# Grouped-query attention on one core: the first load of v issued directly behind the first keys

## The chip, the cores and the metric

The kernel runs on one core of a Trainium2 chip. A core has a matrix engine (TensorE, with a separate row for its weight loads), a vector engine (VectorE), an engine for functions such as exp (ScalarE), a general engine (GpSimd) and one that only issues transfers and waits (SyncE). Each takes its own list of instructions in order; they are tied together by semaphores. Transfers run on 16 DMA engines which all queues share. The metric is the device time of one execution in microseconds; before the change it is 363.3 us, the median of 3 runs (362.96 to 363.51).

## The reference: what is computed

Attention with grouped heads: batch 8, 8 query heads, 2 key and value heads, 1024 positions, head size 64, float32 in and out. Four query heads share one key and value head.

```python
for g in range(n_kv_heads):
    scores = scale * np.matmul(q_group, k_group.transpose(0, 1, 3, 2))
    attn = np.exp(scores - scores_max)
    attn = attn / (np.sum(attn, axis=-1, keepdims=True) + 1e-08)
    output[:, q_start:q_end] = np.matmul(attn, v_group)
```

scale is 1/8, scores_max the maximum of each row.

## The kernel before, in words

**Jobs.** One pair of batch and query head is a job; there are 64, numbered j. A job's scores are computed transposed, in 8 chunks of 128 keys by 1024 queries: two matmuls of 512 columns (L795) fill one PSUM slot `sp` of 128x1024. There are three such slots, so three chunks can be under way.

**Two ways to take the exponential.** Most chunks (378 of 512) go through ScalarE: one instruction (L805) reads a slot and writes exp(scale x score) as bf16 into a tile `pt`. The other 134 go through VectorE, which builds an exponential out of integer operations: a first pass out of PSUM (L816, tile `yt`), then on pairs of chunks the steps L823 (`zt`), L830 (`et`) and L839, with part of L839's columns done by GpSimd (L769). No maximum is subtracted.

**Product with v.** The exponentials are the weights of matmuls against `va`, which holds v as bf16 with a column of ones behind each 64 values, so that the 65th output column is the row sum. L857 does this piece by piece (8 pieces of 128 queries a job); for job 0 alone it goes chunk by chunk (L877), as soon as a chunk's exponential and v are there. Then VectorE takes the reciprocal of the sums (L922) and multiplies (L931), and SyncE stores.

**Where v comes from.** `load_v` (L590) is a transfer on SyncE's queue from v in HBM into a float32 tile `vs`, 256 KB, of which there are two buffers. `place_v` (L595, L596) is a GpSimd copy of `vs` into `va`. There are 16 pairs of batch and key head, so 16 such loads and copies.

**Where q and k come from.** For job 0 they are loaded as float32 by SyncE (k, in two parts, L636 and L638) and by ScalarE's queue (q, L637), cast to bf16 by `place` (L660 on VectorE, L661 on ScalarE), turned by TensorE against an identity (L674, L686) and copied out of PSUM (L691 to L695). For every other job, GpSimd issues a transfer that casts q or k to bf16 in HBM (`cast_q` L563, `cast_k` L576; lines L571 and L579), and SyncE issues a transposing transfer of that into `qt` or `kt` (L614, L604). The casts for jobs 1 to 4 and of the second key head are issued at the start of the kernel, one behind the other.

**What sets the order.** The order of all work is written out beforehand: the class `Plan` plays the engines with fixed costs (the M_ names at the top) and picks, step by step, what TensorE does next. Its list of events, with those for loads and stores sorted in by time, is then emitted, so every engine's list of instructions is fixed before the kernel starts. The plan counts v of job 0 as there at M_V0 = 8000 ns. On TensorE the list begins with idle work on `warm` (L654, L655), the turning of q and k, six chunks of scores of job 0, and then the first 16 products with v (L877); behind these stand the next three chunks of scores, the second of which is the first to read `qt` of job 1.

**Around the change.** The start of the kernel, in program order, is: load k part 1 and part 2 on SyncE with q's load on ScalarE's queue between them, the casting loads of jobs 1 and 2, the idle work, the four `place` casts, and then the first `load_v(0, 0)`. That load carries a dependency added by hand on ScalarE's cast of q:

```python
ins = place(nc.scalar, "q", 0, 2)
...
tc.add_manual_dep(load_v(0, 0).ins, ins.ins.name, Sync, reason="loads in time, not sooner")
```

SyncE's list is therefore: k, k, v, the transposes for jobs 1, 2 and 3, the transpose of the second key head, the second v, and so on. Each transpose waits for its own cast.

Of the kernel before, what the change touches and what calls it, by code (L numbers as in the profile page):

```python
# [486 lines left out]
def kernel(  # L487
# [7 lines left out]
    nc = tc.nc  # L495
# [5 lines left out]
    Sync = mybir.DependencyInfo(mybir.DependencyClass.Sync, mybir.DependencyReason.DATA)  # L501
# [61 lines left out]
    def cast_q(j):  # L563
        b, h = divmod(j, H)
        t = dram.tile([HS, 2 * D], BF16, name=f"qd{j}")
        qd[j] = t
        if j == NJ - 1:
            return nc.gpsimd.dma_start(
                out=t.rearrange("(c p) d -> p c d", p=128), in_=rows(q[b, h], True)
            )  # L570
        return nc.gpsimd.dma_start(  # L571
            out=t.rearrange("(a x) d -> a (x d)", x=4),
            in_=q[b, h].rearrange("(a x) d -> a (x d)", x=8),
        )
# [11 lines left out]
    def rows(x, fours=False):  # L586
        how = "(p c two) d -> p c (two d)" if fours else "(c p two) d -> p c (two d)"
        return x.rearrange(how, p=128, two=2)

    def load_v(b, g):  # L590
        t = vsp.tile([128, NH, 2 * D], FP32, name="vs")
        vs[(b, g)] = t
        return nc.sync.dma_start(out=t, in_=rows(v[b, g], b == g == 0))
# [38 lines left out]
    def load(e, x, lo, hi):  # L632
        src = {"q": q, "k": k}[x][0, 0]
        return e.dma_start(out=f32[x][:, lo:hi], in_=rows(src, True)[:, lo:hi])

    load(nc.sync, "k", 0, 1)  # L636
    load(nc.scalar, "q", 0, NH)  # L637
    load(nc.sync, "k", 1, NH)  # L638
    cast_q(1)
    make_identity(nc, ident)  # L640
    cast_q(2)
# [15 lines left out]
    def place(e, x, lo, hi):  # L657
        to, src = b16[x][:, lo:hi], f32[x][:, lo:hi]
        if e is nc.vector:
            return e.tensor_copy(out=to, in_=src)  # L660
        return e.activation(out=to, in_=src, func=AF.Copy)  # L661

    ins = place(nc.scalar, "q", 0, 2)
    place(nc.vector, "q", 2, NH)
    place(nc.vector, "k", 0, 1)
    place(nc.vector, "k", 1, NH)

    tc.add_manual_dep(load_v(0, 0).ins, ins.ins.name, Sync, reason="loads in time, not sooner")

    s0, s1, s2 = new_slot(0), new_slot(1), new_slot(2)  # L670

# [82 lines left out]
    for when, kind, x, j, c, *cols in ev:  # L754
# [177 lines left out]
        elif kind == "store":  # L932
            b, h = divmod(j, H)
            r = place_of(j * NPIECE)
            ins = nc.sync.dma_start(
                out=rows(out[b, h], j in (0, NJ - 1)),
                in_=ost[:, r : r + NPIECE, :].rearrange("p (s two) d -> p s (two d)", two=2),
            )
# [31 lines left out]
```

The softmax here doesn't subtract the row's maximum and nothing guards it: scores larger than these inputs give would overflow.

## Time and profile before

| what | number |
|---|---|
| time, median of 3 | 363.3 us |
| span of the profiled execution | 362.6 us |
| ScalarE busy | 351.3 us |
| TensorE busy | 350.0 us |
| VectorE busy | 349.8 us |
| GpSimd busy | 125.1 us |
| mean DMA rate | 124 GB/s |

A profile lists for each engine the instructions with their start and length, and for each idle stretch what ended it. A tile is named without its buffer number, so `pt<-sp` is any exp from a PSUM slot. "L805" is line 805 of the kernel. The chain that ended last is followed back from the last instruction, at each step to what released it. DMA queues are numbered: q1 is SyncE's, q10 ScalarE's, q0 GpSimd's casting loads. Busy times of TensorE are modelled from pipelined matmuls and overstate how full it is.

### The profile page before, as it was taken

Reading aid. Unit: us, or ns where it says so; the run is one execution under the profiler, and the core shown is the slowest. Engines: PE = TensorE matmul, PEld = TensorE weight load, DVE = VectorE, ACT = ScalarE, POOL = GpSimd, SP = SyncE. Lnnn points to the kernel's source line nnn. Section 1 sums busy time; section 2 is a strip of 40 time slices with the busy share of each in tenths; the row PEclk is TensorE's granted clock in tenths of the full one; section 3 lists DMA queues with packets and bytes.
Section 4 is the critical chain, followed back from the end, with each engine's and each line's share of the span. In section 5 each row is a group of like instructions: output and inputs, shape, how many; then the busy total and the mean of one; then the engine's idle time right before and its main releaser. Section 6 shows DMA issues by size and latency. Waiting matters only on the chain.

```text
span 362.6 us, 14110 instructions
## 1 busy us (share of the span) xinstructions
PE 350.0 (97%) x6223; PEld 224.6 (62%) x6223; DVE 349.8 (96%) x494; ACT 351.3 (97%) x382; POOL 125.1 (35%) x190
## 2 busy tenths in 40 slices
PE   8789999999999999999999999999999999999995
PEld 3435666666666666656667666666665666666664
DVE  4799999999999999999999999999999999999994
ACT  5799999999999999999999999999999999999995
POOL 3124344353535335342334444244324343421000
PEclk9899999999999999999999999999999999999999
DMA  8625666656668849668466976757488456655132
GB/s 162 117 47 98 128 136 148 119 119 132 134 149 103 169 112 120 140 121 170 111 116 98 171 150 130 125 119 150 107 107 168 110 116 121 149 144 104 47 89 89
DMA packets 89404, 44.82 MB, mean 124 GB/s; under 512 B 46000, under 2 KB 87600, under 8 KB 88112
## 3 DMA queue, kind: packets, MB, share of 16 engines
q1 hardware_dynamic: 86208, 33.44, 41.0%
q0 software_dynamic: 2992, 10.23, 21.1%
q8 instruction: 48, 0.79, 0.9%
q10 hardware_dynamic: 144, 0.26, 0.2%
q14 instruction: 12, 0.10, 0.1%
HBM read 25.17 MB, written 27.00 MB: 144 GB/s over the span
## 4 chain that ended last, share of the span: by engine, by line
DVE 82%; ACT 5%; PE 4%; issue 4%; DMA 2%; POOL 0%; DVEq 0%
DVE yt L816 39%; DVE zt L839 14%; DVE et L830 10%; DVE ost L931 9%; DVE zt L823 9%; ACT pt L805 5%; DVE rec L922 2%; PE sp L795 2%; PE ops L857 2%; DMA vs<-in_v_dram 2%; DMA q<-in_q_dram 1%; PE sp L897 1%; PE ops L877 0%; POOL va L596 0%; ACT q L661 0%
## 5 line engine op out<-in xcount | busy, mean ns | idle before, releaser
L805 ACT ACTIVATE pt<-sp 128x1024 bf16<-128x1024 f32 x378 | 348.7, 1044 | 3.6 <-PE sp L795 3.3
L795 PE MATMUL sp<-qt,kt 64*128 64x512 bf16 x1024 | 174.1, 385 | 5.1 <-ACT pt L805 1.5
L857 PE MATMUL ops<-va,pt 128*128 128x65 bf16 x2928 | 175.9, 194 | 0.0
L816 DVE TENSOR_SCALAR yt<-sp 128x1024 uint16<-128x1024 f32 x134 | 162.8, 1215 | 3.3 <-PE sp L795 3.3
L857 PEld LDWEIGHTS <-pt 128*128 128x128 bf16 x2928 | 130.8, 97 | 33.0 <-issue 33.0
L857 PE MATMUL ops<-va,zt 128*128 128x65 bf16 x1040 | 125.7, 194 | 0.0
L857 PE MATMUL ops<-va,et 128*128 128x65 bf16 x1008 | 119.5, 194 | 0.1
L769 POOL TENSOR_TENSOR zt<-yt,zt 128x320 bf16<-128x320 bf16 x90 | 71.2, 791 | 120.1 <-DVE zt L839 32.9
L857 PEld LDWEIGHTS <-et 128*128 128x128 bf16 x1008 | 81.2, 98 | 21.4 <-issue 21.0
L857 PEld LDWEIGHTS <-zt 128*128 128x128 bf16 x1040 | 84.8, 97 | 10.2 <-issue 10.2
L795 PEld LDWEIGHTS <-kt 64*128 64x128 bf16 x1024 | 48.9, 93 | 57.1 <-issue 36.2
L839 DVE TENSOR_TENSOR zt<-yt,zt 128x1408 bf16<-128x1408 bf16 (+1 forms) x67 | 66.2, 988 | 0.0
L571 POOL DMA_DIRECT2D qd<-in_q_dram x62 | 36.1, 582 | 43.1 <-PE sp L795 39.8
L823 DVE TENSOR_SCALAR zt<-yt 128x2048 uint16<-128x2048 uint16 x67 | 46.2, 690 | 0.4
L830 DVE TENSOR_SCALAR et<-yt 128x2048 uint16<-128x2048 uint16 x67 | 45.5, 679 | 0.0
L931 DVE TENSOR_TENSOR ost<-ops,rec 128x448 f32<-128x448 f32 (+2 forms) x73 | 44.4, 609 | 0.4
L596 POOL CAST va<-vs 128x512 bf16<-128x512 f32 x16 | 10.0, 628 | 28.6 <-DVE ost L931 8.8
L922 DVE RECIPROCAL rec<-ops 128x7 f32<-128x7 f32 (+2 forms) x73 | 14.2, 195 | 0.0
L579 POOL DMA_DIRECT2D kd<-in_k_dram x15 | 8.6, 570 | 11.5 <-PE sp L795 11.5
L649 PE MATMUL ops<-warm 128*128 128x128 bf16 (+1 forms) x63 | 9.2, 265 | 1.2 <-DVE warm L559 1.2
L649 PEld LDWEIGHTS <-warm 128*128 128x128 bf16 x63 | 4.5, 104 | 7.1 <-issue 5.9
L877 PE MATMUL ops<-va,pt 128*128 128x65 bf16 x48 | 2.6, 221 | 2.2 <-POOL va L596 2.2
(37 smaller groups left out, 26.7 us busy)
## 6 DMA issues: line engine op xcount, KB each, us to landing
out_dram<-ost SPq DMA_DIRECT2D x64, 256.0 KB, 3.1
qd<-in_q_dram POOLq DMA_DIRECT2D x63, 128.0 KB, 3.5
vs<-in_v_dram SPq DMA_DIRECT2D x16, 256.0 KB, 3.2
kd<-in_k_dram POOLq DMA_DIRECT2D x15, 128.0 KB, 3.1
kt<-kt SPq DMA_DIRECT2D x30, 64.0 KB, 2.9
qt<-qd SPq DMA_TRANSPOSE x63, 3.9
q<-in_q_dram ACTq DMA_DIRECT2D x1, 256.0 KB, 3.0
kt<-kd SPq DMA_TRANSPOSE x15, 3.8
```

Of the source, the lines that this page charges most:

```text
L571: return nc.gpsimd.dma_start(out=t.rearrange("(a x) d -> a (x d)", x=4), in_=q[b, h].rearrange("(a x) d -> a (x d)", x=8),)
L649: nc.tensor.matmul(ops[bank][:, lo : lo + cols], lhsT=warm[:, 0:128], rhs=warm[:, 0:cols], start=not beside, stop=True, skip_group_check=b ...
L769: gps = nc.gpsimd.tensor_tensor(out=z, in0=flat(yt[j])[:, c, 1024 - GC :], in1=z, op=ALU.mult)
L795: now = nc.tensor.matmul(sps[x][:, half, :], lhsT=t[lo : lo + D, c // NH, ci % NH * 128 : (ci % NH + 1) * 128], rhs=qt[j][lo : lo + D, 0, ...
L805: exps.append(nc.scalar.activation(out=p, in_=where_s[(j, c)], func=AF.Exp, scale=scale))
L816: vec = nc.vector.tensor_scalar(out=yt[ch][:, i, :, :], in0=where_s[c], scalar1=EXP_A, scalar2=EXP_B, op0=ALU.mult, op1=ALU.add,)
L823: vec = nc.vector.tensor_scalar(out=zt[j][:, 0:c], in0=yt[j][:, 0:c], scalar1=0x7F, scalar2=0x3F00, op0=ALU.bitwise_and, op1=ALU.bitwise_or,)
L830: vec = ins = nc.vector.tensor_scalar(out=et[j][:, 0:c], in0=yt[j][:, 0:c], scalar1=0x7F80, scalar2=None, op0=ALU.bitwise_and,)
L839: vec = nc.vector.tensor_tensor(out=z, in0=flat(yt[j])[:, 0:c, 0 : cols[0]], in1=z, op=ALU.mult)
L857: nc.tensor.matmul(ops[plan.group_of[x] % 2][:, lo : lo + D + 1], lhsT=p[:, qs * 128 : (qs + 1) * 128], rhs=va[:, b * G + h // HPG, ci % N ...
L922: vec = nc.vector.reciprocal(out=to, in_=sums)
L931: vec = nc.vector.tensor_tensor(out=to, in0=o, in1=by, op=ALU.mult)
```

## The change

The first load of v is moved up in the program, directly behind the second load of k on SyncE's queue, and loses its dependency on ScalarE's cast. It has nothing left to wait for. The dependency held the load back so that it would not share the DMA engines with the loads of q and k; the change gives that up to have v sooner.

```diff
     load(nc.sync, "k", 0, 1)
     load(nc.scalar, "q", 0, NH)
     load(nc.sync, "k", 1, NH)
+    load_v(0, 0)
     cast_q(1)
     make_identity(nc, ident)
     cast_q(2)
...
-    ins = place(nc.scalar, "q", 0, 2)
+    place(nc.scalar, "q", 0, 2)
     place(nc.vector, "q", 2, NH)
     place(nc.vector, "k", 0, 1)
     place(nc.vector, "k", 1, NH)
-
-    tc.add_manual_dep(load_v(0, 0).ins, ins.ins.name, Sync, reason="loads in time, not sooner")
```

One line fewer: behind L668 every line of the changed kernel has a number smaller by one, and between L639 and L667 the numbers are larger by one.

## The prediction

> **What bounds the kernel now.** I first read the instructions of ScalarE in order of time, because its 351.3 us busy of a 362.6 us span is the largest share. Columns: start, length, engine and line, operation, count, and in brackets the idle time before the stretch with what ended it.
>
> ```profile
> 3.77 0.42 ACT L661 ACTIVATE q<-q 128x256 bf16<-128x256 f32 x1 [1.34 <-DMA q<-in_q_dram]
> ...
> 6.43 3.77 ACT L805 ACTIVATE pt<-sp 128x1024 bf16<-128x1024 f32 x4 [0.62 <-PE sp L795]
> 12.66 47.25 ACT L805 ACTIVATE pt<-sp 128x1024 bf16<-128x1024 f32 x51 [2.46 <-PE sp L795]
> 60.12 297.99 ACT L805 ACTIVATE pt<-sp 128x1024 bf16<-128x1024 f32 x323 [0.20 <-PE sp L795]
> ```
>
> Four exps run, then ScalarE stands still from 10.20 to 12.66, and after that it works without a hole (0.20 us at 60) until 358.1. So the span is the time of the first exp, plus 378 exps back to back at about 0.92 us, plus one hole of 2.46 us, plus a short end. Only the start and that hole can be shortened. VectorE has a hole at the same place: its pass at 13.09 waited 2.57 us for scores, after work that ended at 10.51.
>
> Second, the chain that ended last, in order of time (start, length, what), says where the hole comes from:
>
> ```profile
> 0.74 3.02 DMA q<-in_q_dram
> 3.75 0.02 issue
> 3.77 0.43 ACT q L661
> 4.20 0.02 issue
> 4.22 5.90 DMA vs<-in_v_dram
> 10.11 0.05 issue
> 10.17 0.83 POOL va L596
> 11.00 0.04 issue
> 11.04 1.04 PE ops L877 x16
> 12.08 0.99 PE sp L795 x3
> 13.07 0.02 issue
> 13.09 1.23 DVE yt L816
> ```
>
> The load of the first v tile is issued at 4.22, after ScalarE's first cast, lands 5.9 us later, GpSimd copies it into va, and only then can TensorE run its first 16 products with v (L877). TensorE takes its instructions in order, and behind those 16 stand the next score matmuls (L795) that both ScalarE and VectorE are waiting for.
>
> Third, the waits by engine (total us, times, longest), the first two from the first 45 us, the last from SyncE's own queue, give the sizes:
>
> ```profile
> POOL va L596 <- DMA vs<-in_v_dram: 5.8, 1, 5.8
> ...
> PE ops L877 <- POOL va L596: 2.2, 1, 2.2
> ```
> ```profile
> SPq L593 <- ACT q L661: 2.6, 1, 2.6
> ```
>
> SyncE sat 2.6 us on the dependency that the change removes; TensorE stood 2.23 us before L877, from 8.81 to 11.04.
>
> Fourth, the DMA queues between 5.5 and 7 us (packets, MB, share of the 16 engines):
>
> ```profile
> q0 software_dynamic: 45, 0.19, 101.0%
> ```
>
> q1, SyncE's queue with v on it, moves nothing here although v was issued at 4.22: only q0 does, GpSimd's casting loads (q of heads 1 to 4 and the second k, 128 KB written each). In half-microsecond windows q1's first packets after k come between 7.0 and 7.5. This is why v needed 5.9 us where q and k needed 3.0 and 3.2.
>
> **What the Trainium skill says.** DMA: Bandwidth & Descriptors, section Queues, rings and completion order: an engine takes the descriptors of one ring in order and goes round between the rings that have work, by packets. The trace agrees on the order (v, then the transposes behind it) but shows v kept out for some two microseconds rather than served in turn. The same page, Issuing engines are not separate DMA queues: all queues run on the same 16 engines, so v's bytes are not free wherever they go; the windows from 2 to 4 us show three queues at once, 318 GB/s together. SBUF — State Buffer, section Who interferes with whom: a VectorE instruction with at most one SBUF input outside the two-port modes doesn't contend with GpSimd. The trace agrees: GpSimd's copy of the second v tile at 22.18 lies beside a PSUM pass at 22.04 that takes its usual 1.22 us.
>
> **The change part by part.** Instruction order on all five engines is the same in both kernels; the only difference is that SyncE's third DMA, v, no longer waits for ScalarE.
>
> *Issue of v.* SyncE's two k loads take 0.88 us from 0.74, so v goes out at about 1.62 instead of 4.22: 2.6 us earlier.
>
> *Landing of v.* The trace doesn't show a v load there, so I bound it. Best: 3.0 us as for k and q, landing at 4.6. Worst: 5.9 us again, landing at 7.5. I take about 5.3: v's packets stand directly behind k's in the ring, and k's last pass shortly before 4.0, when the casts have moved only 16 packets; 256 KB at 318 GB/s are 0.8 us, some more for the shared engines. GpSimd is idle from 4.39, its copy is 0.83 us plus 0.1 of hand-over, so va is there at 6.2 (5.5 to 8.4). TensorE wants it at 8.81. Even at the worst bound the whole 2.23 us wait is gone.
>
> *What comes after on TensorE.* 16 products need about 0.5 us at full clock (the third set, at 15.00, was followed by the next work at 15.51), so scores could start at 9.35. Their PSUM slot is freed by the third exp, at 6.43 + 3 x 0.94 = 9.25. From pair start to exp start it took 0.65 us at 12.01, at a granted clock of 0.5; so the fifth exp's scores are ready by 10.0, before ScalarE ends the fourth at 10.20. ScalarE's hole is closed: minus 2.46 us. VectorE's next pass needs the second pair of scores, which can't begin before VectorE's own pass from 8.56 ends at 9.79, and is ready at about 10.3, before VectorE is free at 10.51: its hole closes too. The granted clock, 0.5 between 11 and 13 us after the wait, should also stay at 1, but nothing more is gained by that, for ScalarE never waits again.
>
> *The next input.* That second pair is the first to read qt of head 1, so its transposing load must have landed by 9.8 to 10. Before, it was issued at 4.90 and landed after 5.8 us, at 10.7, standing behind v in the same ring. Now v is out of its way, but the casting load that feeds it (issued 1.25, landed 4.85) shares the engines with v. If v costs it its whole 0.8 us, the transpose goes out at 5.7 and can move when the casts thin out, at about 8; 954 small packets went through from 10 to 11 us, and a transpose has 576 (4032 of under 512 B in the first 30 us, 7 transposes), so one takes some 0.6 us. I take 9.5, bounds 8.2 and 11.5. Head 2's transpose landed at 11.2 and is wanted at about 13.4; later loads are tied to score matmuls and move with them. These cost nothing.
>
> *What v costs at the start.* The first exp depends on q and k. q's 144 packets are all gone by 3.5, before v can move much, and k stands ahead of v in the ring. So the loss is nearly nothing, at worst v's 0.8 us. I take 0.15.
>
> *GpSimd's copy* moves from 10.17 to about 5.3, beside VectorE's casts L692 to L695 and its first pass L816. All read PSUM, and the pass at 22.04 shows such a pass unharmed: nothing.
>
> *Sum.* 2.46 - 0.15 = 2.3 us off a path on which ScalarE has no slack: 363.3 - 2.3 = 361.0, 0.64% less.
>
> **The rivals.**
> 1. *Head 1's qt takes v's place.* For it: it landed at 10.7 before, later than it will be wanted. Against: much of that was v ahead of it. Landing at 10.7 again, the sixth exp's scores, third in TensorE's order, are ready at about 10.7 + 0.45 + 0.2 = 11.35 where ScalarE ends the fifth at 11.12: a hole of 0.2 (VectorE 0.6), so 361.2 to 361.6. At 11.5 it is 1.0: 362.0.
> 2. *k or q is held up* by v's full 0.8 us: 2.46 - 0.8 = 1.7, 361.6. Against: the order in the ring.
> 3. *The gain is given back later*, by loads or buffers that then come late: 363.3. Against: ScalarE's two later stretches show 0.20 us of waiting in 345; everything that feeds it is issued relative to work that shifts along.
> 4. *Slower.* v in front delays k and q by 0.8 and, through the casts, head 1's qt by more than the 2.46 us saved, to beyond 13: no gain and a later start, 363.3 + 0.8 = 364.1. For it: DMA engines are loaded from 2.5 to 11 us. Against: five casts were through by 9.6, and v adds 0.8 us of engine time.
>
> **How the numbers follow.** Forecast 0.65, rival 1 0.18, rival 2 0.06, rival 3 0.06, rival 4 0.05. The forecast itself reaches from 363.3 - 2.46 - 0.2 (the small hole at 60) - 0.3 (spread of the runs of before) = 360.3 up to 361.3; taking in rivals 1 and 2 to 361.9 leaves little over 0.1 outside. Faster by over 0.2% (below 362.57): 0.65 + 0.18 + 0.06 = 0.89; within: 0.06; slower: 0.05.
>
> **What would show it right or wrong.** Right: v issued near 1.6 and landed before 8; no wait of L877 for L596; ScalarE's stretch from about 6.5 going on through 12.66 without a hole over 0.2; first exp at 6.4 to 6.7; the granted clock at 1 from 10 to 14. Wrong by rival 1: a hole of ScalarE or VectorE between 10 and 12 with TensorE waiting at L795 for the load of qt. By rival 2: the casts L660 and L661 later than 3.77 and 3.98. By rival 3: new waits of L805 beyond 13 us. By rival 4: both of the first, and more than 2.5 us of them.

## The result and the profile after

The changed kernel takes 361.1 us (median of 4, 360.94 to 361.45) against 363.36 us before, a ratio of 0.9941 with a 95% interval from 0.9923 to 0.9958. Timed once more in more rounds (first experiment below) it is 0.9945 (0.9933 to 0.9957): 2.0 us less, between 1.6 and 2.4.

ScalarE's instructions of the changed kernel in order of time:

```profile
3.94 0.42 ACT L662 ACTIVATE q<-q 128x256 bf16<-128x256 f32 x1 [1.50 <-DMA q<-in_q_dram]
...
6.29 50.71 ACT L804 ACTIVATE pt<-sp 128x1024 bf16<-128x1024 f32 x55 [0.32 <-PE sp L794]
57.21 297.98 ACT L804 ACTIVATE pt<-sp 128x1024 bf16<-128x1024 f32 x323 [0.20 <-PE sp L794]
```

The 4 and the 51 exps have become one stretch of 55: the hole of 2.46 us is gone, and the small one of 0.20 us has moved from 60.12 to 57.21. q came 0.17 us later than before (3.94 for 3.77), and yet the first exp started 0.14 us earlier (6.29 for 6.43); the first experiment says why.

The chain that ended last, first 10 us of the changed kernel (start, length, what):

```profile
0.74 3.18 DMA q<-in_q_dram
3.91 0.02 issue
3.94 0.43 ACT q L662
4.36 0.05 issue
4.41 0.71 PE sp L673 x5
5.12 0.32 PE ops L673 x3
5.44 0.51 PE ops L685 x8
5.95 0.02 issue
5.98 0.69 DVE kt L694
6.67 1.14 DVE yt L815
7.81 0.04 issue
7.85 0.41 PE sp L794 x2
8.26 0.02 issue
8.28 1.24 DVE yt L815
```

Neither v nor va stands in it any more; it runs from the load of q through the turning of q and k straight into the work. In the waits of the first 45 us (total us, times, longest) nobody waits for L596 now, and the input next in line, the transposed q of head 1, shows a single wait of 0.2 us:

```profile
POOL va L596 <- DMA vs<-in_v_dram: 1.3, 1, 1.3
...
PEld L794 <- DMA qt<-qd: 0.2, 1, 0.2
```

How v got through is in the DMA queues between 4.5 and 5 us of the changed kernel (packets, MB, share of 16 engines):

```profile
q1 hardware_dynamic: 93, 0.18, 94.5%
q0 software_dynamic: 8, 0.03, 32.3%
```

v is 128 packets of 2 KB. Here they pass between 4.0 and 5.5, most of them in the half microsecond shown, in which only 8 of GpSimd's casting packets (q0) start. Before, they passed between 7.0 and 10.

### The profile page after: what moved, and what is told of

It reads as the page before. It is cut to its first block, busy times and chain, and to the rows that moved or that the text cites. A ratio compares the mean times of both kernels' runs of the same rounds, so it can differ in the third digit from the quotient of the medians.

```text
span 359.6 us, 14110 instructions
## 1 busy us (share of the span) xinstructions
PE 348.5 (97%) x6223; PEld 224.1 (62%) x6223; DVE 349.7 (97%) x494; ACT 351.1 (98%) x382; POOL 124.6 (35%) x190
## 4 chain that ended last, share of the span: by engine, by line
DVE 71%; ACT 19%; PE 4%; issue 4%; DMA 1%; DVEq 0%
DVE yt L815 34%; ACT pt L804 19%; DVE zt L838 12%; DVE et L829 8%; DVE ost L930 7%; DVE zt L822 7%; DVE rec L921 2%; PE ops L856 2%; PE sp L794 2%; DMA q<-in_q_dram 1%; PE sp L896 1%; PE sp L673 0%; DVE kt L694 0%; PE ops L685 0%; ACT q L662 0%
## 5 line engine op out<-in xcount | busy, mean ns | idle before, releaser
L856 PE MATMUL ops<-va,pt 128*128 128x65 bf16 x2928 | 176.0, 194 | 0.0
L856 PEld LDWEIGHTS <-zt 128*128 128x128 bf16 x1040 | 84.8, 97 | 10.2 <-issue 10.2
L822 DVE TENSOR_SCALAR zt<-yt 128x2048 uint16<-128x2048 uint16 x67 | 46.2, 689 | 0.4
L596 POOL CAST va<-vs 128x512 bf16<-128x512 f32 x16 | 9.8, 614 | 24.1 <-DVE ost L930 8.8
L843 DVE TENSOR_TENSOR zt<-et,zt 128x2048 bf16<-128x2048 bf16 x3 | 3.7, 1221 | 0.0
```

What stands on the lines that cost most here:

```text
L822: vec = nc.vector.tensor_scalar(out=zt[j][:, 0:c], in0=yt[j][:, 0:c], scalar1=0x7F, scalar2=0x3F00, op0=ALU.bitwise_and, op1=ALU.bitwise_or,)
L856: nc.tensor.matmul(ops[plan.group_of[x] % 2][:, lo : lo + D + 1], lhsT=p[:, qs * 128 : (qs + 1) * 128], rhs=va[:, b * G + h // HPG, ci % N ...
```

## The experiments

Each ratio is against the kernel before as it ran beside the experiment on the same chip: 363.65 us for the changed kernel again and the experiments on the casts, on v's lateness and on v's wait, 363.67 us for the other four timed ones.

### The changed kernel again

No edit.

> The changed kernel once more, timed in more rounds and with a second profile. My theory: the hole of ScalarE (2.46 us) is all there is, so the time is 361.1 again, ratio 0.9935 to 0.9945, and the profiled spans differ by 2.3 to 2.6 us. Rival: the first profile's difference of 3.0 us in span (362.6 to 359.6) is the real gain, because TensorE's clock at the start and after the hole adds 0.5 us; then the ratio is 0.992 and this profile shows the first six score matmuls in 0.8 us again.

Measured: 361.54 us, ratio 0.9945 (0.9933 to 0.9957). First exp at 6.04, no hole, the first six score matmuls in 0.82 us. The ratio is the one my theory named, at the edge of its range. Its second sign failed: the profiled spans differ by 3.2 us (362.6 to 359.4), and the 0.82 us are what the rival had said. In the first profile of before and in that of the changed kernel these matmuls are

```profile
5.78 1.46 PE L795 MATMUL sp<-qt,kt 64*128 64x512 bf16 x6
```
```profile
5.86 0.82 PE L794 MATMUL sp<-qt,kt 64*128 64x512 bf16 x6
```

This isn't the change's doing. In five profiles of kernels that start as before does, the first exp comes at 5.74, 5.98, 6.16, 6.43 and 6.43, and these matmuls take 0.82 to 1.46 us. 1.46 us is also what six of them take behind the hole at a granted clock of 0.5 (at 12.01 in the first profile of before). So the start varies from execution to execution by more than the change moves it.

The 3.0 us between the spans of the first two profiles are explained by which executions were profiled: those took 364.37 and 361.45 us, 2.9 us apart, and the one of before was among its slower ones. A single pair of profiles would have overstated the gain by 0.8 us.

### The kernel before again

No edit; one profile.

> The kernel before once more, for a second profile of it. Theory: the hole of ScalarE near 10 us is there with 2.2 to 2.8 us, v lands after 5.5 us or more; the start of the first exp may differ from the 6.43 us of the first profile by some tenths, as it does between profiles of the changed kernel (6.04 and 6.29). Rival: start and hole are the same in every profile, so that the difference of 3.0 us in span between the first two profiles is what the change is worth.

Measured: 365.31 us. ScalarE in order of time:

```profile
6.43 3.78 ACT L805 ACTIVATE pt<-sp 128x1024 bf16<-128x1024 f32 x4 [0.62 <-PE sp L795]
12.66 1.94 ACT L805 ACTIVATE pt<-sp 128x1024 bf16<-128x1024 f32 x2 [2.46 <-PE sp L795]
15.05 1.94 ACT L805 ACTIVATE pt<-sp 128x1024 bf16<-128x1024 f32 x2 [0.45 <-PE sp L795]
17.35 43.39 ACT L805 ACTIVATE pt<-sp 128x1024 bf16<-128x1024 f32 x47 [0.37 <-PE sp L795]
```

The same hole with the same cause, v landing 6.0 us after its issue. New are two waits behind it, 0.45 and 0.37 us, while TensorE's granted clock stood at 0.5 until 17 us; in the first profile it was back at 1 from 14 on. Over the 42 executions of before that ran beside the second group of experiments, the three with a mean clock of 0.988 took 365.0 to 365.2 us, the twelve with 0.999 or more 362.3 to 363.4. This alone doesn't say which causes which, for a longer hole can also lower the clock.

### Is it the casting loads that hold v up?

v keeps its wait and its issue at 4.2 us; the casting loads of heads 3 and 4 and of the second k are put behind the first score matmul.

```diff
-            ev.append((at - 19000, "ck", None, (b, g), None))
+            ev.append((max(at - 19000, M_START + 200), "ck", None, (b, g), None))
...
-            ev.append((at - 18000, "cq", None, j, None))
+            ev.append((max(at - 18000, M_START + 200), "cq", None, j, None))
```

> As before the change (v waits for ScalarE's cast and is issued at 4.2), but the casting loads of heads 3 and 4 and of the second k are issued behind the first score matmul and GpSimd's copy of v, instead of at 2.9 to 4.4 us. Theory: v was slow because these casts held the engines; now it takes 3 to 4 us, lands by 8, and the hole closes: 361.0 to 361.4. Rival: v is slow on this queue at that time whatever else moves (5.5 us or more, landing near 10), and the time stays at 363.3.

Measured: 361.37 us, ratio 0.9945 (0.9932 to 0.9958). GpSimd and ScalarE in order of time:

```profile
7.24 0.61 POOL L596 CAST va<-vs 128x512 bf16<-128x512 f32 x1 [4.29 <-DMA vs<-in_v_dram]
```
```profile
5.98 50.69 ACT L805 ACTIVATE pt<-sp 128x1024 bf16<-128x1024 f32 x55 [0.40 <-PE sp L795]
```

v takes 3.0 us, lands at 7.2, and the hole is gone without v being issued any earlier. So it was neither SyncE's queue nor the issue time as such: v was slow because it came behind casting loads. Its first packets come between 5.0 and 5.5 here, where they came between 7.0 and 7.5 before. What in the casting loads does it, their bytes, their packets or their number, no run separates. Head 1's transpose, still behind v in the ring, now lands 2.9 us after its issue instead of 5.8. The whole gain of the change can be had from the other side.

### How late may v be?

v waits for the fourth idle matmul of TensorE (the expectation calls it the third; the issue came at 3.11).

```diff
-    load_v(0, 0)
...
-    dummy(6, HS)
+    dummy(3, HS)
+    third = nc.tensor.matmul(
+        ops[1][:, 0:HS], lhsT=warm[:, 0:128], rhs=warm, start=True, stop=True
+    )
+    tc.add_manual_dep(load_v(0, 0).ins, third.ins.name, Sync, reason="v a little later")
+    dummy(2, HS)
```

> As changed, but v is issued only when the third idle matmul of TensorE is done, at about 2.9 us instead of 1.7: later than the loads of q and k need the engines, earlier than before (4.2). Theory: q and k land 0.15 us earlier than in the changed kernel, v lands by 8 at the latest and the hole stays closed, 361.0, no different from the changed kernel. Rival (the casting loads keep out whatever comes behind them in time): v takes 5 us or more again, lands after 8.2, and a hole of up to 1 us opens, 361.5 to 362.

Measured: 361.78 us, ratio 0.9957 (0.994 to 0.9975), in two groups: 12 of 16 executions took 361.2 to 361.9, 4 took 363.1 to 364.6. The profiled one was of the four; ScalarE in it:

```profile
5.80 3.77 ACT L808 ACTIVATE pt<-sp 128x1024 bf16<-128x1024 f32 x4 [0.18 <-PE sp L798]
12.60 1.94 ACT L808 ACTIVATE pt<-sp 128x1024 bf16<-128x1024 f32 x2 [3.02 <-PE sp L798]
```

v landed after 7.2 us, at 10.3. Its packets began at 5.0 and 113 of the 128 were through by 7, but the last four came between 9.5 and 10. A second profile was taken to see the other group.

> The kernel with v issued at 3.1 us once more, for a second profile: 12 of its 16 timed executions took 361.2 to 361.9 us, 4 took 363.1 to 364.6, and the profile taken was one of the four. Theory (at this issue time v and the casting loads race for the DMA engines, and v either gets in before them or waits them out): a fast execution shows v landing by 7.5 and no hole, with everything else alike. Rival (the two groups differ in TensorE's clock and not in v): v lands after 9 again and the hole is there, whatever the time.

Measured: 361.65 us. GpSimd and ScalarE:

```profile
8.15 0.61 POOL L596 CAST va<-vs 128x512 bf16<-128x512 f32 x1 [3.73 <-DMA vs<-in_v_dram]
```
```profile
6.10 51.13 ACT L808 ACTIVATE pt<-sp 128x1024 bf16<-128x1024 f32 x55 [0.40 <-PE sp L798]
```

v landed after 5.0 us, at 8.1, its last packet before 8; ScalarE has no hole. v came later than either theory had it (8 and 7.5), and TensorE waited 0.3 us for it. Both of my answers were half right: at 3.1 us v got through in time in one profile, and in the other a few last packets were late and cost the whole hole. That the other three slow executions had the same cause is likely but not shown. The issue at 1.7 has margin, 2.3 us between the end of GpSimd's copy at 6.3 and TensorE's first use at 8.61; 3.1 has not.

### v's wait without v's place in the ring

In the kernel before, GpSimd's first copy reads the tile of zeros `warm` instead of the loaded v, so the values of v for the first four heads of batch 0 are left out. v's load itself stays where it was, ahead of head 1's transpose.

```diff
-            in_=vs.pop((b, g)).rearrange(
+            in_=(warm.rearrange("p (c e) -> p c e", c=NH) if b == g == 0 else vs.pop((b, g))).rearrange(
```

> As before the change, with v's load where it was, but GpSimd fills the first part of va from a tile of zeros and so waits for no load: the products with v of the first four heads are left out in value, not in work. v still stands in the ring ahead of head 1's transpose. Theory (the wait for v is the only thing in the hole, head 1's transpose hardly counts): head 1's qt lands at 10.7 as before, ScalarE's hole shrinks from 2.46 to about 0.2 and VectorE's to 0.6, 361.2 to 361.5. Rival (the changed kernel gains as much by freeing head 1's transpose from v as by v itself): a hole of 1 us or more stays, 362.2 or more.

Measured: 362.32 us, ratio 0.9961 (0.9947 to 0.9975). Waits of the first 13 us, then ScalarE in order of time:

```profile
PEld L795 <- DMA qt<-qd: 1.5, 1, 1.5
DVE yt L816 <- PE sp L795: 1.5, 2, 1.0
...
PE sp L795 <- DMA qt<-qd: 1.2, 1, 1.2
```
```profile
6.16 4.69 ACT L805 ACTIVATE pt<-sp 128x1024 bf16<-128x1024 f32 x5 [0.33 <-PE sp L795]
11.32 46.54 ACT L805 ACTIVATE pt<-sp 128x1024 bf16<-128x1024 f32 x50 [0.48 <-PE sp L795]
```

The time and VectorE's wait are nearer to the rival, though v is still the larger part. With v out of the way as a value, head 1's transposed q is what TensorE waits for, until 10.68, and VectorE stands 1.0 us, ScalarE 0.48. Of the 2.0 us that the change brings, some 1.4 are v's wait (0.0039 of 363.65) and the rest, 0.6, is head 1's transpose, which landed 5.7 us after its issue here and 4.4 in the changed kernel, where v no longer stands ahead of it. The medians give 1.3 and 0.8. The two intervals overlap, so the split is rough; the new wait itself is shown.

### What guards the start: v ahead of k

```diff
+    load_v(0, 0)
     load(nc.sync, "k", 0, 1)
...
     load(nc.sync, "k", 1, NH)
-    load_v(0, 0)
```

> As changed, but v's load stands ahead of both loads of k on SyncE's queue, so it is issued at 0.7 us and k at 1.2 and 1.6. Theory (standing behind k is what keeps the start unharmed): k lands at 4.4 to 5.0 instead of 4.1, q some tenths later, the first exp starts 0.5 to 1.0 us later than in the changed kernel, and the time is 361.8 to 362.5; no hole. Rival (the place in the ring doesn't matter, the engines have room for all three): the same as the changed kernel, 361.1 to 361.6.

Measured: 363.4 us, ratio 0.9995 (0.9981 to 1.0009). VectorE's casts and ScalarE's first exps in order of time:

```profile
4.73 0.30 DVE L661 CAST q<-q 128x256 bf16<-128x256 f32 x1 [3.02 <-DMA q<-in_q_dram]
5.08 0.56 DVE L661 CAST k<-k 128x128 bf16<-128x128 f32 x1
6.11 0.36 DVE L661 CAST k<-k 128x384 bf16<-128x384 f32 x1 [0.48 <-DMA k<-in_k_dram]
```
```profile
8.17 3.98 ACT L804 ACTIVATE pt<-sp 128x1024 bf16<-128x1024 f32 x4 [0.62 <-PE sp L794]
```

There is no hole but one of 0.23 us at 12.4, and yet the whole gain is gone: q lands 0.8 us later than in the changed kernel, k's second part at 6.1, and the first exp starts at 8.17 instead of 6.29. The loss, 1.9 us, is about double what I expected. In this profile, of an execution of 363.9 us, TensorE is also slower until 12 us (16 products take 1.06 us, in the changed kernel 0.67), so not all that it shows is the loads.

### v beside k, on ScalarE's queue

```diff
-    load_v(0, 0)
+    load_v(0, 0, nc.scalar)
```

with the engine as a new argument of `load_v`; the load is issued at 1.15 us, right behind q.

> As changed, but v's first load is issued on ScalarE's queue right behind q, with no wait, so it stands behind q and beside k instead of behind k. Theory (only what stands ahead of v in its own ring is shielded; another ring shares): q lands as in the changed kernel, k lands 0.2 to 0.5 us later, the first exp starts 0.2 to 0.5 us later, 361.4 to 361.9; v lands before 6 and no hole opens. Rival (the early issue is all that counts): the same as the changed kernel within 0.2 us.

Measured: 362.79 us, ratio 0.9974 (0.9962 to 0.9986). VectorE and ScalarE:

```profile
3.79 0.29 DVE L661 CAST q<-q 128x256 bf16<-128x256 f32 x1 [2.08 <-DMA q<-in_q_dram]
4.00 0.22 DVE L661 CAST k<-k 128x128 bf16<-128x128 f32 x1
5.06 0.68 DVE L661 CAST k<-k 128x384 bf16<-128x384 f32 x1 [0.83 <-DMA k<-in_k_dram]
```
```profile
6.84 50.70 ACT L804 ACTIVATE pt<-sp 128x1024 bf16<-128x1024 f32 x55 [0.18 <-PE sp L794]
```

q, ahead of v in the same ring, lands as before; the second part of k, in another ring, is the one held up, and the first exp is 0.55 us later than in the changed kernel's first profile, 0.8 later than in its second. The direction is that of the theory, the size larger. The profiled execution, 362.0 us, is among the fastest of the 21, which reach from 361.9 to 363.8, so the 1.25 us that the median loses is only in part explained by it.

### The clock behind the hole

Nine idle matmuls are put ahead of the first product with v in the kernel before.

```diff
             if first:
+                dummy(9, HS)
                 new_bank(0)
```

> As before the change, with nine idle matmuls of 512 columns ahead of the first product with v, so that TensorE isn't idle while it waits. Theory (the halved clock behind the hole costs ScalarE some tenths: eight exps there took 0.3 us longer than elsewhere): the granted clock stays at 1 from 10 to 14 us, the hole stays near 2.4 us less some tenths, and the time is 0.2 to 0.5 us below before. Rival (the clock costs nothing, as I wrote): the exps behind the hole follow each other no faster, the time is that of before within 0.1%.

Measured: 363.46 us, ratio 0.9995 (0.9983 to 1.0007). ScalarE:

```profile
5.74 3.77 ACT L805 ACTIVATE pt<-sp 128x1024 bf16<-128x1024 f32 x4 [0.22 <-PE sp L795]
12.15 47.04 ACT L805 ACTIVATE pt<-sp 128x1024 bf16<-128x1024 f32 x51 [2.64 <-PE sp L795]
```

The clock stayed at 1 from 9 to 16 us, its mean is 0.997 or more in all 14 executions, and in the profile the exps behind the hole run at full pace (47.04 us for 51, where the first profile of before has 47.25 and the second 48.1 with its two waits). In the times this can't be told from nothing. In this profile v landed at 10.46, 0.3 us later than in the first profile of before, so part may have been lost there; what the clock alone is worth in the times stays open between 0.6 us saved and 0.3 lost. The profile shows where the clock enters the hole:

```profile
11.13 0.66 PE L878 MATMUL ops<-va,pt 128*128 128x65 bf16 x16 [0.96 <-POOL va L596]
```

From the first product to the next exp it is 1.02 us here (11.13 to 12.15) and 1.62 in the first profile of before (11.04 to 12.66), where the same 16 products took 1.04. So some 0.6 us of the 2.46 us hole were TensorE's halved clock, which the wait itself had brought about. And a first exp 0.7 us earlier (5.74 for 6.43) only made the hole longer: its end came earlier by the faster work behind v's landing, not by the earlier start.

### Both cures at once

The change and the later casting loads together.

```diff
     load(nc.sync, "k", 1, NH)
+    load_v(0, 0)
...
-            ev.append((at - 18000, "cq", None, j, None))
+            ev.append((max(at - 18000, M_START + 200), "cq", None, j, None))
```

(and the same for "ck").

> The change together with the later casting loads of heads 3 and 4 and the second k (issued behind the first score matmul). Theory: both close the same hole, and nothing is left to gain there: the same time as either alone, 361.1 to 361.5. Rival: the casts still cost the loads of q and k something at the start, so a further 0.2 us or more comes off, 361.0 or less.

Measured: 361.58 us, ratio 0.995 (0.9932 to 0.9967). ScalarE has one stretch again, from 6.31 on. Nothing is added that could be told from noise: both cures close the same hole. No version was found that beats the changed kernel.

## Why the prediction was right, point by point

The time (361.0 forecast, 361.1 measured) and the mechanism were right; some of its terms were not what they seemed, and that the sum came so close is in part luck (point 5).

1. *Issue and landing of v.* Forecast 1.62 and 5.3 (4.6 to 7.5); measured 1.68 and, after 3.9 us, 5.6. The reason given, casting loads that keep v out, was argued then and is shown now by moving three of the five casts alone.
2. *TensorE's wait.* Forecast to vanish at either bound. It did: L876 starts at 8.61 behind the scores, without a wait.
3. *Head 1's transpose.* Forecast to land at 9.5, wanted by 9.8 to 10; it was issued at 5.04 and landed at 9.44. TensorE's weight load stood 0.2 us for it and VectorE not at all (its pass starts at 10.15, when L822 is done). Rival 1 was thus not met, but it was closer than its 0.18 said: with v still ahead in the ring it is real, and there I had sized it too small, 361.2 to 361.6 where 362.3 was measured. I had let ScalarE's hole be 0.2 us and it was 0.48, VectorE's 0.6 and it was 1.0. I had also priced it by ScalarE, and VectorE's wait is the one that counts: the chain that ended last runs for 82% of the span of before on VectorE and for 5% on ScalarE. VectorE's third pass starts 0.96 us later than in the changed kernel (11.11 for 10.15), and the profiled execution is 0.87 us longer (362.32 for 361.45).
4. *What v costs at the start.* Forecast 0.15 us; q and k came 0.17 us later in one profile and 0.12 in the other. But the first exp, forecast for 6.4 to 6.7, came at 6.29 and 6.04, earlier than the 6.43 of before: how fast TensorE turns q and k and makes the first scores differs by more than this term. The reason for the small loss, that v stands behind k in the ring, holds: the Trainium skill's DMA: Bandwidth & Descriptors, section Queues, rings and completion order, has descriptors of one ring taken in order, and the runs with v ahead of k and beside it lose 1.9 and 0.5 to 0.8 us at the first exp. The worst bound of 0.8 us, v's bytes at the rate seen, was not reached behind k. As a price of v standing in the way it is too low: k's second part was cast at 6.1 instead of about 4.4 when v went first, 1.7 us later, of which 0.45 us is its later issue.
5. *The sum, 2.46 - 0.15.* It came out near the measured 2.0 to 2.3, but it isn't how the time is made up. Before, the end of the hole hung on v's landing and the work behind it, so the start didn't enter; after, with the hole gone, ScalarE's work follows its first exp. In the first two profiles the fifth exp starts at 12.66 and at 9.98 (6.29 + 4 x 0.922), 2.68 us apart, and the next 51 run 0.23 us faster: 2.91 in all, and the two executions differ by 2.92 us. But that execution of before took 364.37 us, 1.1 more than the median from which I subtracted its hole. A median execution must lose less at that place than 2.46 us and the slower exps behind it; that the forecast lands on the measured gain all the same is luck.
6. *The clock gains nothing more.* Too strong: two profiles of before show ScalarE slower or waiting behind the hole at a clock of 0.5, and some 0.6 us of the hole itself goes with it. In the times it isn't shown.
7. *GpSimd's copy beside VectorE's PSUM casts.* Forecast at no cost. Of these casts only L694 (L695 before) lies beside the copy, and it takes 0.69 us as before. The copy itself became shorter, 0.61 for 0.83 us, away from L823, which reads and writes SBUF; two copies as late as before's but not beside L823, at 10.33 with v issued at 3.1 and at 10.46 in the run on the clock, took 0.61 too. This fits the Trainium skill's SBUF — State Buffer, section Who interferes with whom: a vector instruction in a two-port mode, as L823's kind can be, and a GpSimd one shut each other out. Which mode L823 ran in, the trace doesn't tell. The runs with v ahead of k and beside it show a cost that I hadn't thought of: there the copy comes first, at 4.94 and 4.91, and VectorE's cast of k beside it, from SBUF to SBUF, takes 0.56 us instead of 0.22 (128x128) and 0.68 instead of 0.36 (128x384). So a part of what those two places lose is not the transfer but the copy of v.
8. *Rivals 2, 3 and 4* were not met in size: casts of q and k later than before, which was the sign of rival 2, but by less than 0.2 us of its 0.8, and no wait of ScalarE beyond 13 us but the 0.20.

## What to carry to other kernels

Where one engine runs almost without a hole from its start to the end, look for the one place where it stands, follow the chain back to a transfer, and ask what that transfer stood behind, not only when it was issued. A load has a right place: behind what the start needs in the same ring, ahead of the bulk that isn't needed yet; here a place ahead of k cost the whole gain, one in another ring more than half of it, and a place 1.4 us later made it a matter of luck. A wait removed also moves whatever stood behind the waiting transfer, and that second effect was roughly a third of the gain here.

## What the runs showed that I had not expected

- A load of 256 KB took 3.0, 3.9, 5.0, 5.9 or 7.2 us from issue to landing in these kernels, by what else was under way; in the last, 113 of 128 packets were through by 7 us and the last four came at 9.5 to 10.
- The granted clock fell to 0.5 after TensorE had been idle for less than 2 us (from 8.81; it averaged 0.78 between 10 and 11 us in one profile, 0.58 in another, and 0.5 from 11 on, so it fell at about 10.6 and 10.2), though the whole wait was 2.2 us. It came back at 14.0 us in one execution and at 17.0 in the other: 3.4 us at half clock in one, 6.8, twice as long, in the other.
- On one chip the kernel before spreads over 362.5 to 365.2 us in 27 executions, the changed one over 361.18 to 361.73 in five: as is to be expected where the time no longer hangs on v's landing.
